# Two-layer hybrid trunk on one core: earlier activation table, MLP weights split in units of 1024 columns, weight pools by phase, odd heads' softmax transposes one step later

## The chip, the cores and the metric

The kernel runs on one core of a Trainium2 chip. The metric is the device time in microseconds (us) of one execution; lower is better. The kernel before has a median of 2300.85 us over 3 runs. PE is TensorE, DVE VectorE, ACT ScalarE, POOL GpSimd, SP the engine that issues the DMAs.

## The reference

The input x has 256 tokens of width 2048; everything is in float32. Layer 0 mixes with 8 heads of differential attention and 8 heads of a gated delta rule, layer 1 with 16 heads of dilated attention, and each layer ends in an MLP of width 8192.

```
x = x + diff_delta_mixer(rms_norm(x, ab_norm))      # layer 0: proj = h @ w_in, then heads, then @ w_out
x = x + square(relu(rms_norm(x, mlp_norm[0]) @ w1[0])) @ w2[0]
x = x + dilated_mixer(rms_norm(x, c_norm))          # layer 1
x = x + square(relu(rms_norm(x, mlp_norm[1]) @ w1[1])) @ w2[1]
```

## The kernel before, in words

**Dense products.** All products with weights go through `dense` (L189 to L211): 512 output columns (or fewer) for 256 tokens, contracted over 16 blocks `kc` of 128. PE multiplies fp32r numbers, so each fp32 weight is split: ACT rounds it to a high part (`S.copy`, L201, a CAST in the trace), DVE subtracts that from the original for the low part (`tt`, L202, shown as L107), and each `kc` takes, for either half of the tokens, three matmuls: high by high (L206), low weight by high input (L207), high weight by low input (L208). That is 96 matmuls in a dense. `wload` (L171) fetches weights in pieces of 512 KB, two `kc` each, with 4 buffers; the split parts have 6 buffers each of one `kc`, all in one pool `wp` that lives through the program.

**Phases.** Layer 0's mixer runs the denses b0, z2, bv0, b1, z0, av0, a0 and so on, one for each group of heads, then `wo`, the output product, in two parts for the two kinds of heads, over four blocks of columns (wo00 to wo03, wo10 to wo13). An MLP has 4 groups, each of 4 denses up (m_0 to m_3, by `w1`) and 4 down (n_0 to n_3, by `w2`). Behind an up dense comes relu (two ACT instructions), the square in place, 16 DVE transposes (`turn_quadrant`, L283), and the split of the result into `hh` (ACT, L314) and `hl` (DVE): n_0 needs m_3's as the last four `kc`. Layer 1's mixer has c0 to c7 and cv0 to cv3, a head pair e0 to e7 for each c, and the output product co. In the trace an MLP dense m_0 stands for every m of index 0, whatever its layer and group.

**The order of the work.** The work beside the denses is written as generators in three queues, "g", "s" and "o". `drip()` (L182) takes one step of "g" or "s", in turn, after each `kc` of a dense, and one of "o" after every fourth. A `yield` in a generator so moves what follows it two `kc` on. The instructions of each engine are then ordered by the scheduler of the language from this program order, the weight casts ahead of others (`tc.high_priority`).

**The norm.** `stats_block` (L247) sums the squares of x on ACT; `rstd` is applied to the products, so it is wanted only at the end of the first dense. `xt_block` (L257) turns x by 8 PE transposes for 512 columns (`xa0` to `xa3` at the start, `xb3`, `xc3`, `xd3` for the last block at the later phase starts, where the other blocks come during the phase before), and splits it into `xh` and `xl`.

**Heads of layer 1.** `c_side` (L1019) takes one head pair through norm, transposes, scores, softmax (`sm`), PE transposes of the softmax (`e1pt`) with a copy on ACT, and the product with v (`e1po`). Even pairs run in queue "g", odd ones in "s" (L1111).

Of the kernel before, what the change touches and what calls it, by code (L numbers as in the profile page):

```python
# [19 lines left out]
P = 128  # L20
# [11 lines left out]
AHEAD = 60  # L32
# [55 lines left out]
def trunk(  # L88
# [5 lines left out]
    V, S, G, E = nc.vector, nc.scalar, nc.gpsimd, nc.tensor  # L94

    cp = ctx.enter_context(tc.tile_pool(name="cp", bufs=1))
    sp = ctx.enter_context(tc.tile_pool(name="sp", bufs=2))
    wp = ctx.enter_context(tc.tile_pool(name="wp", bufs=6))
    xp = ctx.enter_context(tc.tile_pool(name="xp", bufs=4))
    dp = ctx.enter_context(tc.tile_pool(name="dp", bufs=1, space=bass.MemoryType.DRAM))  # L100
    psd = ctx.enter_context(tc.tile_pool(name="psd", bufs=4, space=PSUM))
# [4 lines left out]
    def tt(o, a, b, op):  # L106
        V.tensor_tensor(out=o, in0=a, in1=b, op=op)  # L107
# [13 lines left out]
    def act(o, a, f, scale=1.0, bias=0.0, accum=None):  # L121
        if accum is None:
            S.activation(out=o, in_=a, func=f, scale=scale, bias=bias)  # L123
        else:
            S.activation(out=o, in_=a, func=f, scale=scale, bias=bias, accum_out=accum)
# [7 lines left out]
    def ps_m(name):  # L133
        return psm.tile([P, 512], F32, tag="m", name=name)
# [34 lines left out]


    def wload(wsrc, k0, nm):  # L171
        raw = wp.tile([P, 2, 512], F32, tag="wr", name=f"{nm}r{k0}", bufs=4)
        off = 0
        for s in wsrc:
            m = s.shape[1]
            nc.sync.dma_start(raw[:, :, off:off + m], s[k0 * P:(k0 + 2) * P, :].rearrange("(c p) n -> p c n", p=P))
            off += m
        return raw
# [7 lines left out]
            step("o")  # L186
        tick[0] += 1

    def dense(wsrc, stat, kcs, nm, pre=(), every=1):  # L189

        n = sum(s.shape[1] for s in wsrc)
        ps = [psd.tile([P, 512], F32, tag="d", name=f"{nm}p{h}") for h in range(NH)]
        first, last = kcs[0], kcs[-1]
        for j, kc in enumerate(kcs):
            if j % 2 == 0:
                raw = pre[j // 2] if j // 2 < len(pre) else wload(wsrc, kc, nm)
            w = raw[:, j % 2, :n]
            wh = wp.tile([P, 512], F32R, tag="wh", name=f"{nm}h{kc}")[:, :n]
            wl = wp.tile([P, 512], F32R, tag="wl", name=f"{nm}l{kc}")[:, :n]
            with tc.high_priority(offset=AHEAD):  # L200
                S.copy(wh, w)  # L201
                tt(wl, w, wh.bitcast(F32), ALU.subtract)  # L202
            for h in range(NH):
                sh, sl = stat(kc, h)
                o = ps[h][:, :n]
                E.matmul(o, lhsT=sh, rhs=wh, start=kc == first, stop=False)  # L206
                E.matmul(o, lhsT=sh, rhs=wl, start=False, stop=False)  # L207
                E.matmul(o, lhsT=sl, rhs=wh, start=False, stop=kc == last)  # L208
            if j % every == 0:
                drip()  # L210
        return ps  # L211
# [7 lines left out]
    KC16 = list(range(16))  # L219
# [8 lines left out]
    ident = cst("ident")  # L228
# [74 lines left out]
    def mlp(layer, blocks, hp, done):  # L303
        w1, w2 = mlp_w1[layer], mlp_w2[layer]
        stat = stat_of(blocks)

        def spread(r, nm, hb):
            hT = hp.tile([P, 4, T], F32, tag="hT", name=nm + "hT", bufs=2)
            for i in range(4):
                turn_quadrant(r, hT, i)  # L310
                yield
            hh = hp.tile([P, 4, T], F32R, tag="hh", name=nm + "hh")
            hl = hp.tile([P, 4, T], F32R, tag="hl", name=nm + "hl")
            S.copy(hh, hT)  # L314
            tt(hl, hT, hh.bitcast(F32), ALU.subtract)
            hb.append((hh, hl))
            yield

        for g in range(4):
            hb = []  # L320
            for b in range(4):
                nm = f"m{layer}_{g}_{b}"
                c0 = (g * 4 + b) * 512
                ps = dense([w1[:, c0:c0 + 512]], stat, KC16, nm)
                r = hp.tile([P, NH, 512], F32, tag="hr", name=nm + "r", bufs=2)
                for h in range(NH):
                    act(r[:, h, :], ps[h], AF.Relu, scale=rstd[:, h:h + 1])
                act(r, r, AF.Square)
                streams["s"].append(spread(r, nm, hb))
            hstat = stat_of(hb)  # L330
            for n in range(4):
                ps = dense([w2[g * 2048:(g + 1) * 2048, n * 512:(n + 1) * 512]], hstat, KC16, f"n{layer}_{g}_{n}")
                add_to_x(n, ps)
                if g == 3:
                    done(n)
# [13 lines left out]
    warm = sp.tile([P, 512], F32, tag="junk", name="warm")  # L349
    V.memset(warm, 0.0)  # L350
    pw = ps_m("pw")
    for n in range(NWARM):
        E.matmul(pw[:, :P], lhsT=warm[:, :P], rhs=warm[:, :P], start=True, stop=True)
    xq = [x_tile(n, "xq") for n in range(4)]
    pre = []
    for n in range(4):
# [7 lines left out]
        if n < 3:  # L364
            pre.append(wload(b_cols(0), 2 * n, "b0"))
    with ExitStack() as mix:
        op = mix.enter_context(tc.tile_pool(name="op", bufs=1))
        mp = mix.enter_context(tc.tile_pool(name="mp", bufs=1))

# [11 lines left out]
        for n in range(4):  # L381
            for _ in xt_block(xq[n], n, 0, f"xa{n}", xb):
                pass


        cga = cp.tile([P, NH, 2, 64], F32, name="cga")
# [12 lines left out]
                    tt(sg[:, h, qk, hd:], rt[:, h, 1, :], g1, ALU.mult)  # L399

        def init():
            for n in range(4):
                stats_block(xq[n], n, f"xas{n}")
                yield
            stats_end("xast")
            ts(rhalf, rstd, 0.5, None, ALU.mult)
# [552 lines left out]
        ps = dense([win[:, 6920:7184]], xstat, KC16, "z2", every=2)  # L959
# [11 lines left out]
        ps = dense([win[:, 6144:6656]], xstat, KC16, "z0")  # L971
# [7 lines left out]
        ps = dense([win[:, 6656:6920]], xstat, KC16, "z1", every=2)  # L979
# [24 lines left out]


    cb = []
    with tc.tile_pool(name="hp0", bufs=6) as hp:
        mlp(0, nb, hp, lambda n: streams["s"].append(next_norm(n, 2, f"xc{n}", cb, hp)))


    cin = c_w_in[0]
    cstat = stat_of(cb)
    with ExitStack() as mix:
        op1 = mix.enter_context(tc.tile_pool(name="oq", bufs=1))
        mp1 = mix.enter_context(tc.tile_pool(name="mq", bufs=1))
        oc = [None] * 8
# [2 lines left out]
        def c_side(r, s, nm):  # L1019
            w = "gs"[s % 2]  # L1020
# [21 lines left out]
            for e in range(2):  # L1042
# [61 lines left out]
        for s in range(8):  # L1104
            ps = dense([cin[:, s * 256:(s + 1) * 256], cin[:, 2048 + s * 256:2304 + s * 256]], cstat, KC16, f"c{s}")
# [6 lines left out]
            if s % 2 == 0:  # L1112
                g = s // 2
# [24 lines left out]
        for h in range(NH):  # L1138
            nc.sync.dma_start(ov[:, h, n * 512:(n + 1) * 512], xs[n][:, h, :])

    with tc.tile_pool(name="hp1", bufs=6) as hp:
        mlp(1, nb1, hp, done1)


# [23 lines left out]
```

## Time and profile before

| | us |
|---|---|
| median of 3 runs (2300.76 to 2300.91) | 2300.85 |
| profiled execution, device time | 2301.12 |
| its span in the trace | 2299.3 |
| PE busy | 2280.7 |
| DVE busy | 1732.9 |
| ACT busy | 1275.7 |

The span is the time from the first to the last event of the trace; the profiled execution's device time lies 1.8 above it. The busy times of the engines overlap. PE's granted clock shows as 9 in all 40 slices of the page, so any lower clock is short.

### The profile page before, as it was taken

How to read it: one execution, taken by the hardware profiler on the slowest of the kernel's cores; microseconds unless marked ns; L12 is line 12 of the kernel's file. 1: busy time of each engine (PE TensorE's matmuls, PEld its weight loads, DVE VectorE, ACT ScalarE, POOL GpSimd, SP SyncE). 2: the span in 40 equal slices, each digit the busy share in tenths (PEclk: the TensorE clock that was granted, in tenths of full speed). 3: DMA queues.
4: the chain of work that ended last, by engine and by line, in shares of the span. 5: the costliest groups of instructions: out<-in, count | busy, mean ns of one | idle time of the engine just before them, and what ended most of it. 6: DMA issues, size and time to landing. Idle time of an engine off the chain costs nothing.

```text
span 2299.3 us, 31489 instructions
## 1 busy us (share of the span) xinstructions
PE 2280.7 (99%) x10536; PEld 1889.1 (82%) x10536; DVE 1732.9 (75%) x3539; ACT 1275.7 (55%) x2376; POOL 5.6 (0%) x15
## 2 busy tenths in 40 slices
PE   9999999999999999999999999999999999999999
PEld 8888888788888888888888888888888888888887
DVE  6768787867857857857898888987775775775774
ACT  6656756765545545545555565556554554554553
POOL 0000000000000000000000000000000000000000
PEclk9999999999999999999999999999999999999999
DMA  7655464566666666666656555555666666666665
GB/s 251 179 172 167 142 182 140 160 183 182 202 192 183 202 194 188 196 194 189 194 187 201 177 167 174 174 178 177 193 193 193 193 192 193 188 197 194 183 211 163
DMA packets 264775, 426.65 MB, mean 186 GB/s; under 512 B 22514, under 2 KB 94372, under 8 KB 264612
## 3 DMA queue, kind: packets, MB, share of 16 engines
q1 hardware_dynamic: 255812, 420.04, 59.9%
q10 hardware_dynamic: 8800, 4.60, 0.8%
q8 instruction: 82, 1.34, 0.2%
q14 instruction: 81, 0.66, 0.1%
HBM read 420.11 MB, written 4.46 MB: 185 GB/s over the span
## 4 chain that ended last, share of the span: by engine, by line
PE 84%; DVE 10%; ACT 2%; issue 2%; DMA 1%; ACTq 0%; SPq 0%; DVEq 0%
PE m_0p L208 3%; PE m_0p L206 3%; PE m_1p L208 3%; PE m_2p L208 3%; PE n_1p L208 3%; PE n_2p L208 3%; PE m_0p L207 3%; PE n_2p L207 3%; PE n_2p L206 3%; PE n_1p L207 3%; PE m_2p L207 3%; PE m_1p L206 3%; PE m_2p L206 3%; PE n_1p L206 3%; PE m_1p L207 3%; PE n_3p L208 3%
## 5 line engine op out<-in xcount | busy, mean ns | idle before, releaser
L107 DVE TENSOR_TENSOR n_3l<-n_3r,n_3h 128x512 fp32r<-128x512 f32 x128 | 88.3, 691 | 68.3 <-ACT n_3h L201 68.1
L107 DVE TENSOR_TENSOR n_2l<-n_2r,n_2h 128x512 fp32r<-128x512 f32 x128 | 88.2, 691 | 68.3 <-ACT n_2h L201 68.1
L107 DVE TENSOR_TENSOR m_0l<-m_0r,m_0h 128x512 fp32r<-128x512 f32 x128 | 88.4, 691 | 66.3 <-ACT m_0h L201 66.1
L201 ACT CAST n_3h<-n_3r 128x512 fp32r<-128x512 f32 x128 | 79.7, 623 | 89.3 <-DVE n_3l L107 73.6
L201 ACT CAST n_2h<-n_2r 128x512 fp32r<-128x512 f32 x128 | 79.7, 623 | 89.3 <-DVE n_2l L107 73.6
L107 DVE TENSOR_TENSOR n_1l<-n_1r,n_1h 128x512 fp32r<-128x512 f32 x128 | 87.0, 690 | 51.6 <-ACT n_1h L201 51.4
L201 ACT CAST m_0h<-m_0r 128x512 fp32r<-128x512 f32 x128 | 79.7, 623 | 81.8 <-DVE m_0l L107 61.8
L201 ACT CAST n_1h<-n_1r 128x512 fp32r<-128x512 f32 x128 | 78.9, 623 | 77.7 <-DVE n_1l L107 58.1
L201 ACT CAST m_1h<-m_1r 128x512 fp32r<-128x512 f32 x128 | 78.1, 622 | 64.6 <-PE m_1p L208 35.3
L107 DVE TENSOR_TENSOR m_1l<-m_1r,m_1h 128x512 fp32r<-128x512 f32 x128 | 87.1, 691 | 33.7 <-ACT m_1h L201 31.9
L201 ACT CAST m_3h<-m_3r 128x512 fp32r<-128x512 f32 x128 | 77.0, 621 | 47.0 <-PE m_3p L208 35.0
L201 ACT CAST m_2h<-m_2r 128x512 fp32r<-128x512 f32 x128 | 77.0, 621 | 46.8 <-PE m_2p L208 35.3
L201 ACT CAST n_0h<-n_0r 128x512 fp32r<-128x512 f32 x128 | 77.0, 621 | 46.5 <-PE n_0p L208 35.3
L107 DVE TENSOR_TENSOR m_3l<-m_3r,m_3h 128x512 fp32r<-128x512 f32 x128 | 84.9, 689 | 11.6 <-ACT m_3h L201 9.9
L107 DVE TENSOR_TENSOR m_2l<-m_2r,m_2h 128x512 fp32r<-128x512 f32 x128 | 84.9, 690 | 11.2 <-ACT m_2h L201 9.5
L107 DVE TENSOR_TENSOR n_0l<-n_0r,n_0h 128x512 fp32r<-128x512 f32 x128 | 84.9, 689 | 11.0 <-ACT n_0h L201 9.2
L289 DVE STREAM_TRANSPOSE m_0hT<-m_0r 32x256 f32<-32x256 f32 x128 | 55.8, 436 | 10.5 <-ACT m_0r L123 8.0
L289 DVE STREAM_TRANSPOSE m_1hT<-m_1r 32x256 f32<-32x256 f32 x128 | 55.8, 436 | 10.4 <-ACT m_1r L123 7.9
L289 DVE STREAM_TRANSPOSE m_3hT<-m_3r 32x256 f32<-32x256 f32 x128 | 55.8, 436 | 10.4 <-ACT m_3r L123 7.9
L289 DVE STREAM_TRANSPOSE m_2hT<-m_2r 32x256 f32<-32x256 f32 x128 | 55.8, 436 | 10.4 <-ACT m_2r L123 7.9
L208 PE MATMUL n_0p<-n_0h,m_3hl 128*128 128x512 f32 x64 | 25.8, 404 | 1.9 <-DVE m_3hl L107 1.9
L206 PE MATMUL n_0p<-n_0h,m_3hh 128*128 128x512 f32 x64 | 25.0, 390 | 0.0
(2552 smaller groups left out, 7389.0 us busy)
## 6 DMA issues: line engine op xcount, KB each, us to landing
m_0r<-in_mlp_w_dram SPq DMA_DIRECT2D x64, 512.0 KB
m_1r<-in_mlp_w_dram SPq DMA_DIRECT2D x64, 512.0 KB
m_2r<-in_mlp_w_dram SPq DMA_DIRECT2D x64, 512.0 KB
m_3r<-in_mlp_w_dram SPq DMA_DIRECT2D x64, 512.0 KB
n_0r<-in_mlp_w_dram SPq DMA_DIRECT2D x64, 512.0 KB
n_1r<-in_mlp_w_dram SPq DMA_DIRECT2D x64, 512.0 KB
n_2r<-in_mlp_w_dram SPq DMA_DIRECT2D x64, 512.0 KB
n_3r<-in_mlp_w_dram SPq DMA_DIRECT2D x64, 512.0 KB
```

Of the source, the lines that this page charges most:

```text
L107: V.tensor_tensor(out=o, in0=a, in1=b, op=op)
L201: S.copy(wh, w)
L206: E.matmul(o, lhsT=sh, rhs=wh, start=kc == first, stop=False)
L207: E.matmul(o, lhsT=sh, rhs=wl, start=False, stop=False)
L208: E.matmul(o, lhsT=sl, rhs=wh, start=False, stop=kc == last)
L289: V.transpose(out=dv[:, :, :, q], in_=sv[:, :, :, j, :])
```

## The change

1. Right after the memset of `warm`, ACT does a small Square on it (`awarm`); the activation table that it shares with the later activations is so loaded in front of it.
2. Behind the transposes of x's first block PE does 4 more matmuls into `pw`, with a result that nothing reads.
3. `init()` in queue "s" starts with two steps that do nothing, and its squares are placed behind the last weight cast issued by then (`tc.issue_after`). Everything behind `init` in "s" moves two steps on, its DMAs of constants included.
4. The MLP's denses split weights in units of 2 `kc`: CAST and subtraction of 1024 columns, with 3 buffers each instead of 6.
5. The buffers of the split weights move from `wp` to a pool of each phase: `wq0` (mixer of layer 0), `wq1` (its MLP), `wq2` and `wq3` (layer 1).
6. Odd head pairs of layer 1 yield once more in front of the transposes of the softmax.

```diff
     def wload(wsrc, k0, nm):
-        raw = wp.tile([P, 2, 512], F32, tag="wr", name=f"{nm}r{k0}", bufs=4)
+        raw = wp.tile([P, 2, 512], F32, tag="wr", name=f"{nm}r{k0}")
...
+    wq, cast = [None], [None]
+
+    def dense(wsrc, stat, kcs, nm, pre=(), every=1, unit=1):
...
-            w = raw[:, j % 2, :n]
-            wh = wp.tile([P, 512], F32R, tag="wh", name=f"{nm}h{kc}")[:, :n]
-            wl = wp.tile([P, 512], F32R, tag="wl", name=f"{nm}l{kc}")[:, :n]
-            with tc.high_priority(offset=AHEAD):
-                S.copy(wh, w)
-                tt(wl, w, wh.bitcast(F32), ALU.subtract)
+            if j % unit == 0:
+                w = raw[:, j % 2:j % 2 + unit, :n]
+                whs = wq[0].tile([P, unit, 512], F32R, tag="wh", name=f"{nm}h{kc}", bufs=6 // unit)[:, :, :n]
+                wls = wq[0].tile([P, unit, 512], F32R, tag="wl", name=f"{nm}l{kc}", bufs=6 // unit)[:, :, :n]
+                with tc.high_priority(offset=AHEAD):
+                    cast[0] = S.copy(whs, w)
+                    tt(wls, w, whs.bitcast(F32), ALU.subtract)
+            wh, wl = whs[:, j % unit], wls[:, j % unit]
...
-                ps = dense([w1[:, c0:c0 + 512]], stat, KC16, nm)
+                ps = dense([w1[:, c0:c0 + 512]], stat, KC16, nm, unit=2)
...
+    act(sp.tile([P, 16], F32, tag="rs_z", name="awarm"), warm[:, :16], AF.Square)
...
+        wq[0] = mix.enter_context(tc.tile_pool(name="wq0", bufs=1))
...
+            if n == 0:
+
+                for _ in range(4):
+                    E.matmul(pw[:, :P], lhsT=ident, rhs=xq[0][:, 1, 256:384], start=True, stop=True)
...
         def init():
+            yield
+            yield
             for n in range(4):
-                stats_block(xq[n], n, f"xas{n}")
+
+                with tc.issue_after(cast[0].ins):
+                    stats_block(xq[n], n, f"xas{n}")
                 yield
...
-    with tc.tile_pool(name="hp0", bufs=6) as hp:
+    with tc.tile_pool(name="wq1", bufs=1) as wq[0], tc.tile_pool(name="hp0", bufs=6) as hp:
...
             yield
+            if w == "s":
+                yield
             pT = mp1.tile([P, 2, 384], F32, tag="c_pT" + w, name=nm + "pT")
```

The call for `w2` gets `unit=2` too, and `wq2` and `wq3` are made like `wq0` and `wq1`.

ACT at the start, before (xas0j is the square, xa0h the rounding of x's first block, b0h the first weights; a number behind a name tells buffers apart):

```order
L125 ACT_TABLE_LOAD
L125 ACTIVATE xas0j_249,ssqp<-xq_101 128x512
L123 ACTIVATE xa0h<-xa0t_136,gt 128x256
L201 CAST b0h_229<-b0r_109 128x512
L201 CAST b0h_239<-b0r_109 128x512
L123 ACTIVATE xa0h<-xa0t_136,gt 128x256
```

ACT at the start with the change:

```order
L123 ACT_TABLE_LOAD
L123 ACTIVATE awarm<-warm 128x16
L123 ACTIVATE xa0h<-xa0t_141,gt 128x256
L123 ACTIVATE xa0h<-xa0t_150,gt 128x256
L123 ACTIVATE xa0h<-xa0t_141,gt 128x256
L204 CAST b0h_238<-b0r_111 128x512
L204 CAST b0h_248<-b0r_111 128x512
```

The table load and a small Square now stand in front, the two squares of x's first block are gone from here, and three xa0h stand ahead of the first cast instead of one.

PE where the first mixer ends (wo13, its last output block) and the first MLP begins (m_0_0), before:

```order
L208 MATMUL wo13p_5730<-wo13h_5833,d3ol 128x512
L206 MATMUL m_0_0p_5850<-m_0_0h_5854,xb0h 128x512
L207 MATMUL m_0_0p_5850<-m_0_0l_5855,xb0h 128x512
...
L207 MATMUL m_0_0p_5851<-m_0_0l_5865,xb0h 128x512
L208 MATMUL m_0_0p_5851<-m_0_0h_5864,xb0l 128x512
L231 MATMUL xb3t_5880<-ca,xs_4992 128x128 x4
L206 MATMUL m_0_0p_5850<-m_0_0h_5891,xb0h 128x512
```

The same place with the change; xb3t are the transposes of the last block of x:

```order
L212 MATMUL wo13p_5739<-wo13h_5842,d3ol 128x512
L235 MATMUL xb3t_5889<-ca,xs_5035 128x128
L235 MATMUL xb3t_5916<-ca,xs_5035 128x128
L235 MATMUL xb3t_5889<-ca,xs_5035 128x128 x3
L210 MATMUL m_0_0p_5863<-m_0_0h_5867,xb0h 128x512
L210 MATMUL m_0_0p_5864<-m_0_0h_5867,xb0h 128x512
L235 MATMUL xb3t_5916<-ca,xs_5035 128x128 x3
L211 MATMUL m_0_0p_5863<-m_0_0l_5868,xb0h 128x512
L212 MATMUL m_0_0p_5863<-m_0_0h_5867,xb0l 128x512
L211 MATMUL m_0_0p_5864<-m_0_0l_5868,xb0h 128x512
```

The transposes, which came after the 12th matmul of m_0 before, now come right behind wo13's last, with two high-by-high matmuls in their midst, and the first matmul with a low part of the weights (L211) follows them.

PE at the softmax transposes of head pair e1, before (cv1 is the dense that runs there, 12 of its matmuls follow e1pt, then e1po and the next dense c3):

```order
L208 MATMUL cv1p_13076<-cv1h_13295,xc3l 128x512
L231 MATMUL e1pt_13306<-ca,e1sm_13202 128x128 x3
L231 MATMUL e1pt_13311<-ca,e1sm_13239 128x128 x3
L206 MATMUL cv1p_13075<-cv1h_13318,xc3h 128x512
L207 MATMUL cv1p_13075<-cv1l_13319,xc3h 128x512
...
L208 MATMUL cv1p_13076<-cv1h_13332,xc3l 128x512
L1078 MATMUL e1po<-e1pT,vc_12596 128x256
L1079 MATMUL e1po<-e1pT,vc_12596 128x128
```

The same with the change:

```order
L210 MATMUL cv1p_12069<-cv1h_12314,xc3h 128x512
L211 MATMUL cv1p_12069<-cv1l_12315,xc3h 128x512
L212 MATMUL cv1p_12069<-cv1h_12314,xc3l 128x512
L235 MATMUL e1pt_12325<-ca,e1sm_12195 128x128 x3
L235 MATMUL e1pt_12330<-ca,e1sm_12232 128x128 x3
L210 MATMUL c3p_12338<-c3h_12343,xc0h 128x512
L211 MATMUL c3p_12338<-c3l_12344,xc0h 128x512
```

The transposes moved behind cv1's last 12 matmuls; c3 follows them, and e1po comes within c3. It is the same with e3 and e5.

Three more places of the changed order, in words. In n_0 DVE gets, between m_3r's square and m_3hl, 4 transposes, a subtraction of 1024 columns, 5 transposes, a subtraction, 4, one, 3, one, and then m_3hl. The first cast into a new pool waits for PE's last matmul of the phase before. At the end of the first mixer, g3's output product g3po and wo10's first matmul stand 75 rows of PE apart instead of 104, and on SP's queue three loads of wo10's weights now come ahead of the two DMAs that load blocks 2 and 3 of x again (`xs`), which wait for g3's output; DVE adds wo02 and wo03 into them, and so frees the PSUM banks that wo10 and wo11 take.

## Rows read from the trace of the kernel before

**Rows 1.** The page, section 1: busy time in us, share of the span and instructions of each engine.

```profile
PE 2280.7 (99%) x10536; PEld 1889.1 (82%) x10536; DVE 1732.9 (75%) x3539; ACT 1275.7 (55%) x2376; POOL 5.6 (0%) x15
```

**Rows 2.** PE's waits over the whole span: what waited, for what, us in total, times, the longest in us.

```profile
PE b0p L206 <- ACT b0h L201: 2.3, 1, 2.3
PE n_0p L208 <- DVE m_3hl L107: 1.9, 8, 0.2
PE e3pt L231 <- DVE e3sm L117: 1.5, 1, 1.5
PE e1pt L231 <- DVE e1sm L117: 1.5, 1, 1.5
PE e5pt L231 <- DVE e5sm L117: 1.5, 1, 1.5
...
PE bv0v L231 <- DVE bv0a L113: 1.0, 1, 1.0
...
PE g1kt L231 <- DVE g1kh L117: 0.3, 1, 0.3
```

**Rows 3.** Timeline of PE, the first matmul of some phases: z2 (the phase behind b0), m_0 and m_1 of layer 0's first group, n_0 of that group (599.67), and n_0, n_1, n_2 of the second. The columns of a timeline are start us, duration us, engine, line, operation, out<-in, shapes and count, and in brackets the engine's idle time before it and what ended that.

```profile
36.55 0.28 PE L206 MATMUL z2p<-z2h,xa0h 128*128 128x264 f32 x1
...
511.64 0.39 PE L206 MATMUL m_0p<-m_0h,xb0h 128*128 128x512 f32 x1
...
534.39 0.39 PE L206 MATMUL m_1p<-m_1h,xb0h 128*128 128x512 f32 x1
...
599.67 0.39 PE L206 MATMUL n_0p<-n_0h,m_0hh 128*128 128x512 f32 x1
...
774.29 0.39 PE L206 MATMUL n_0p<-n_0h,m_0hh 128*128 128x512 f32 x1
...
796.59 0.39 PE L206 MATMUL n_1p<-n_1h,m_0hh 128*128 128x512 f32 x1
...
818.35 0.39 PE L206 MATMUL n_2p<-n_2h,m_0hh 128*128 128x512 f32 x1
```

**Rows 4.** Timeline of the start, PE and ACT (xq is the block of x, xa0t its transposes, xas0j its square, b0h the rounded weights).

```profile
6.00 1.28 ACT L125 ACT_TABLE_LOAD   x1 [6.00 <-DMA xq<-in_x_dram]
...
6.05 0.63 PE L231 MATMUL xa0t<-ca,xq 128*128 128x128 f32 x4 [0.18 <-DMA xq<-in_x_dram]
...
7.29 0.63 ACT L125 ACTIVATE xas0j<-xq 128x512 f32<-128x512 f32 x1
...
8.28 1.12 ACT L201 CAST b0h<-b0r 128x512 fp32r<-128x512 f32 x2
...
8.94 0.79 PE L206 MATMUL b0p<-b0h,xa0h 128*128 128x512 f32 x1 [2.26 <-ACT b0h L201]
```

**Rows 5.** Windows: start:end and length in us, then busy us (and instructions) of PE, PEld, DVE, ACT and POOL, then the granted clock of PE (1.00 is 2.4 GHz), the share of the DMA engines and GB/s. One of the start, and the two that make up b0.

```profile
7.00:8.00 1.00, 0.00 (x0) 0.00 (x0) 0.00 (x0) 0.99 (x4) 0.00 (x0) 1.00 0.97 337
...
8.94:15.06 6.12, 6.12 (x16) 4.72 (x17) 4.41 (x8) 4.28 (x11) 0.00 (x0) 0.50 1.06 377
...
15.06:36.55 21.49, 21.49 (x105) 17.65 (x104) 17.28 (x62) 15.83 (x40) 0.00 (x0) 1.00 0.66 206
```

**Rows 6.** Windows, as above: the stretch before e3pt in which PE waits.

```profile
1397.35:1398.86 1.51, 0.00 (x0) 0.00 (x0) 1.40 (x6) 1.51 (x4) 0.00 (x0) 1.00 0.90 281
```

**Rows 7.** Groups by line and shape: line, engine, operation, out<-in, shapes and count, busy us and mean ns of one, and the idle time before them with what ended it. m_3l is the low part of the weights, m_3hh and m_3hl are the two parts of the squared activations, m_0hT their transpose.

```profile
L314 ACT CAST m_3hh<-m_3hT 128x1024 fp32r<-128x1024 f32 x8 | 8.4, 1053 | 24.8 <-DVE m_3hT L289 24.8
...
L107 DVE TENSOR_TENSOR m_3l<-m_3r,m_3h 128x512 fp32r<-128x512 f32 x128 | 84.9, 689 | 11.6 <-ACT m_3h L201 9.9
...
L107 DVE TENSOR_TENSOR m_3hl<-m_3hT,m_3hh 128x1024 fp32r<-128x1024 f32 x8 | 9.8, 1225 | 3.2 <-ACT m_3hh L314 3.2
...
L289 DVE STREAM_TRANSPOSE m_0hT<-m_0r 32x256 f32<-32x256 f32 x128 | 55.8, 436 | 10.5 <-ACT m_0r L123 8.0
```

**Rows 8.** Timeline of PE around e3's softmax transposes.

```profile
1396.86 0.49 PE L231 MATMUL e3pt<-ca,e3sm 128*128 128x128 f32 x3
...
1398.86 0.70 PE L231 MATMUL e3pt<-ca,e3sm 128*128 128x128 f32 x3 [1.51 <-DVE e3sm L117]
```

**Rows 9.** Timeline of PE, n_0 in the first group of layer 0, where it first needs m_3hl.

```profile
616.22 0.39 PE L207 MATMUL n_0p<-n_0l,m_3hh 128*128 128x512 f32 x1
...
616.84 0.50 PE L208 MATMUL n_0p<-n_0h,m_3hl 128*128 128x512 f32 x1 [0.24 <-DVE m_3hl L107]
```

**Rows 10.** Timeline at n_0's start in the second group: the last matmul of m_3, a weight cast on ACT, the square of m_3r.

```profile
774.06 0.39 PE L208 MATMUL m_3p<-m_3h,xb3l 128*128 128x512 f32 x1
...
774.49 0.62 ACT L201 CAST n_0h<-n_0r 128x512 fp32r<-128x512 f32 x1
...
775.73 1.06 ACT L123 ACTIVATE m_3r<-m_3r 128x1024 f32<-128x1024 f32 x1
```

**Rows 11.** Timeline at the step from the MLP of layer 0 to the mixer of layer 1, PE.

```profile
1210.88 0.39 PE L208 MATMUL n_3p<-n_3h,m_3hl 128*128 128x512 f32 x1
...
1211.10 0.39 PE L206 MATMUL c0p<-c0h,xc0h 128*128 128x512 f32 x1
```

**Rows 12.** Timelines of PE and DVE before wo10: g3's output product, DVE's second add of wo02 into xs, wo10's first matmul.

```profile
440.29 1.10 PE L766 MATMUL g3po<-g3u,g3aT 128*128 128x128 f32 x8
...
456.45 0.69 DVE L107 TENSOR_TENSOR xs<-wo02p,xs 128x512 f32<-128x512 f32 x1
...
465.18 0.39 PE L206 MATMUL wo10p<-wo10h,g2oh 128*128 128x512 f32 x1
```

More of the change, by code (lines that the diff above doesn't have):

```diff
@@ L97, in trunk @@
     sp = ctx.enter_context(tc.tile_pool(name="sp", bufs=2))
-    wp = ctx.enter_context(tc.tile_pool(name="wp", bufs=6))
+    wp = ctx.enter_context(tc.tile_pool(name="wp", bufs=4))
     xp = ctx.enter_context(tc.tile_pool(name="xp", bufs=4))
@@ L187, in drip @@
         tick[0] += 1
-    def dense(wsrc, stat, kcs, nm, pre=(), every=1):
+    wq, cast = [None], [None]
+    def dense(wsrc, stat, kcs, nm, pre=(), every=1, unit=1):
         n = sum(s.shape[1] for s in wsrc)
@@ L331, in mlp @@
             for n in range(4):
-                ps = dense([w2[g * 2048:(g + 1) * 2048, n * 512:(n + 1) * 512]], hstat, KC16, f"n{layer}_{g}_{n}")
+                ps = dense([w2[g * 2048:(g + 1) * 2048, n * 512:(n + 1) * 512]], hstat, KC16, f"n{layer}_{g}_{n}", unit=2)
                 add_to_x(n, ps)
@@ L1013, in trunk @@
     with ExitStack() as mix:
+        wq[0] = mix.enter_context(tc.tile_pool(name="wq2", bufs=1))
         op1 = mix.enter_context(tc.tile_pool(name="oq", bufs=1))
@@ L1139, in done1 @@
             nc.sync.dma_start(ov[:, h, n * 512:(n + 1) * 512], xs[n][:, h, :])
-    with tc.tile_pool(name="hp1", bufs=6) as hp:
+    with tc.tile_pool(name="wq3", bufs=1) as wq[0], tc.tile_pool(name="hp1", bufs=6) as hp:
         mlp(1, nb1, hp, done1)
```

## The prediction, on record before the change was run

> **What bounds the kernel now.** I read the page's head first: TensorE (PE) is busy for 2280.7 of 2299.3 us, so only what keeps PE from starting its next matmul counts, and time saved on VectorE (DVE, 1732.9) or ScalarE (ACT, 1275.7) counts only where PE waits for it [rows 1]. Then the list of PE's waits: the reader is to see that they are few and short, and that the largest ones lie at the start (b0p), in the attention heads (e1pt, e3pt, e5pt) and in the dense n_0 [rows 2]. The timeline gives the price of each, since a wait shows less than it costs. The steady pace is the yardstick: n_1 to n_2 start 818.35 - 796.59 = 21.76 us apart, one dense of 96 matmuls at .2266 each [rows 3]. The profiled execution took 2301.12 us, .27 above the median of 2300.85; the sum is made against 2301.12.
>
> **The start.** Before b0p, PE stands from 6.67 to 8.94, 2.26 us. The reader is to see ACT filling that time: table load from 6.00 for 1.28, the square xas0j at 7.29, the rounding of xa0, the cast at 8.28, then PE [rows 4]. In the windows the granted clock is 1.00 from 7 to 8; the 6.12 us from 8.94 on run at 0.50, that is 1.2 GHz, after that pause of 2.26, and the rest of b0 at 1.00 [rows 5]. Pauses of 1.51 us did not lower it: 1.00 in the one of e3pt [rows 6]. b0 takes 36.55 - 8.94 = 27.61 [rows 3, 4]; at full clock it would be 21.76 plus 24 transposes (xa1 to xa3) of .124. The .124 is m_0's excess, 534.39 - 511.64 - 21.76 = .99, over its 8 transposes [rows 3]. That is 24.73, so 2.88 are lost.
> The change loads the table during the first input transfer, and its ACT order is three xa0h and then the cast. The cast then waits for its data only: 512 KB at 337 GB/s is 1.5 us [rows 5], behind the x half that releases PE at 6.05 [rows 4], so 7.55. A cast of .62 [rows 10] brings the first matmul to about 8.2, and gains .7. The 4 added matmuls are like the four xa0t in .63 [rows 4]; they lie in a pause that ends with the cast, and cost nothing while the cast is later than 7.3. PE then pauses about .9 us, to 8.2, less than the 1.51 that kept the clock, so I take the 2.88 as gained too. Against this, b0's second operand and the x blocks come no earlier than their transfers: .3 by choice, as the smallest wait of that kind between engines in the list, g1kt [rows 2]. **Start: -3.3** (from -.4, with the clock lost again, to -3.6). The squares moved behind the casts (8 of .63, 5.0 us of ACT [rows 4]) are wanted only when b0 ends near 36, and z2 after it has banks of its own; if that cover failed, the next phase would wait.
>
> **Odd heads.** e3pt's first three transposes start at 1396.86 and the next at 1398.86; without a wait that would be .33 later (3 of .11, .49 for three with the tail), so 1.67 each is lost for a wait shown as 1.51 [rows 2, 8]. One more yield puts them 12 matmuls (2.7 us) later, past the softmax's end, in e1, e3 and e5 alike. The ACT copy and the product e1po behind them slip equally, into the next dense, where ACT (55% busy) has room. **-5.0** (from -4.5, the waits as shown).
>
> **MLP in units of 1024 columns.** n_0 lasts 796.59 - 774.29 = 22.30, .54 over the pace, in 8 groups [rows 3]. The cause: the first matmul with m_3hl starts at 616.84 instead of .23 after its neighbour, at 616.45 [rows 9]. The changed DVE order has, between the squared m_3r and m_3hl, 16 transposes and 4 subtractions of 1024 columns, so 16 x .436 + 4 x 1.225 + 1.225 for m_3hl itself = 13.1 [rows 7]. ACT now has a cast of 1.05 instead of .62 in front of the square, which ended at 775.73 + 1.06, so m_3r is ready near 777.25 and m_3hl near 790.4 [rows 7, 10]. PE wants it 16.78 after n_0's start (616.45 - 599.67), at 791.07 [rows 3, 9]. The wait goes, with .7 to spare: **-4.3** (8 x .54; nothing if it stays). What is late next is the pair of casts itself: the first kc of a pair is ready .43 + .53, about 1 us, later than a single one. The three buffers hold the same 6 kc, and in the order the tightest pair (the one of kc 10) keeps 1.35 us. The 8 casts and 8 subtractions saved per dense are off the bound: 0.
>
> **The pools by phase.** The first write to a new pool waits for the last reader of the old one, the last matmul. Before, c0p follows n_3p by .22 [rows 11]. Now, with T the start of that matmul, a cast begins at T+.43 (as n_0h does after m_3p [rows 10]). For m_0 of both layers the cast (1.05) is done at T+1.49, the subtraction (1.22) at T+2.77 and PE goes on at T+2.81. Meanwhile it does the tail .23, 8 transposes (.99) and 2 matmuls (.45), which the order now puts there: 1.14 lost each. For c0 in 512 columns, behind DVE's add into xs (.69 [rows 12]), PE goes on at about T+1.9 with 1.3 of work: .6. **+2.9** (from 0, if the release comes without a wait, to 6.8 if nothing fits beside: 2 x 2.58 + 1.61).
>
> **The first mixer.** All of its "s" stream slips two steps, transfers of constants included. PE's seven waits there, from bv0v's 1.0 to g1kt's .3, 4.2 in all [rows 2], may go or return elsewhere: 0, from -4.2 to +4. One place worse than before is told as a rival.
>
> Sum: -3.3 - 5.0 - 4.3 + 2.9 + 0 = -9.7, or 2301.1 - 9.7 = 2291.4 as profiled and **2291.2** against the median.
>
> **Rivals.** *The clock falls at the start anyway.* For it: it fell after 2.26 us of pause, and no row shows one of .9 there, right after PE's first few us. Then the 2.9 return: 2294.1. Beside the row stands a rule of the Trainium skill, "TensorE: Matmul & The Clock Gate", Part 1, "What's actually happening": the slow clock is the default, and a monitor grants the fast one by how busy PE has recently been. By that rule a start with few matmuls may fall back even after a short pause, and the sum would be this rival's; the trace agrees that PE's recent activity matters, with 0.50 after the pause at the start.
> *The change does not do what it says in n_0.* If the transposes or the pair of kc 12 come .7 later than worked out, the old wait stays: 2295.5.
> *New waits take back most of it.* xs is reloaded only after g3's output: in before g3po starts at 440.29, the second add into the reloaded xs at 456.45, and wo10p, which needs the bank that this add frees, at 465.18, 24.9 after g3po [rows 12]. In the changed order only 75 instead of 104 matmuls lie between, 17 us at .2266, against a chain of 16.8 (456.45 + .69 - 440.29), and three weight loads now stand ahead of the reload on SP's queue (up to 4.7 us, 3 x 512 KB at 337 GB/s [rows 5]). In time they give from nothing to 4.5 late. With the pools at their upper bound (+3.9) that is at most 2299.6, at half of both 2295.4; I take 2297.5, within .2%.
> *The pairs do not keep up, and the kernel is slower.* If the 1024-column chain comes more than the 1.35 us late, all 64 denses wait, not 8: at n_0's .54 each 34.6, of which 4.3 are paid today; the start, the heads and the pools still give -5.4, so 2301.1 + 34.6 - 4.3 - 5.4 = **2326**. For it: the chain of cast and subtraction grows from 1.3 to 2.3 us. Against it: DVE is busy 75% and gets 1.2 us back per dense, ACT 1.5 (8 x (2 x .689 - 1.225) and 8 x (2 x .62 - 1.053) [rows 7, 10]).
>
> **How the numbers follow.** What a measurement can tell from no change is .2%, 4.6 us: faster means below 2296.25. Forecast .60 (2288 to 2294); clock .17; n_0 as before .06; new waits .11; slower .06. Faster gets the forecast, n_0 and most of the clock's case, .81; within .2% the new waits and the rest, .13; slower .06. The range goes down to 2286.5 (the mixer's -4.2 and part of the pools' +2.9 saved) and up to 2299 (new waits near their bound); outside it lie the slower case and some .05 to .1 of tails.
>
> **What would show it.** Right: PEclk 1.00 from 8 to 16 and the first b0p near 8.2; no e1pt, e3pt, e5pt and no m_3hl in the list of PE's waits; n_0 at 21.8; new waits of .5 to .7 for m_0h, m_0l, c0l at the three phase starts. Wrong: a clock of 0.5 after b0p, n_0 still at 22.3, any dense of the MLP besides m_0 above 21.8, or a wait at wo10p.

## The result, and the profile after

The changed kernel takes 2304.06 us, the median of 22 runs (2299.87 to 2307.01), beside 2300.88 of the kernel before (22 runs, 2298.07 to 2302.36). The ratio is 1.0015, with a 95% interval of 1.0008 to 1.0021: a little slower, though within the .2% that the prediction counts as no change. The forecast was 2291.2, in a range to 2299.0: wrong, and on the wrong side. The profiled execution took 2305.11 us, 1.0 above the median.

PE's waits in the changed kernel (what waited for what, us in total, times, the longest) show a swap. The rows of e1pt, e3pt, e5pt and of n_0's m_3hl [rows 2] are gone, as forecast. At the head stand av1p and wo00p, denses of the first mixer that wait for the low part of their weights, and d0at and d2po of its heads; none of them stood in the list before.

```profile
PE av1p L211 <- DVE av1l L107: 3.2, 2, 2.8
PE wo00p L211 <- DVE wo00l L107: 1.9, 1, 1.9
PE d0at L235 <- DVE d0aa L113: 1.6, 2, 1.2
...
PE d2po L926 <- DVE d2mx L903: 1.1, 1, 1.1
PE b0p L210 <- ACT b0h L204: 0.8, 1, 0.8
...
PE m_0p L211 <- DVE m_0l L107: 0.4, 2, 0.2
```

The first matmuls of some phases (the timeline's columns are as in [rows 3]) give each stage its sum:

```profile
8.37 0.73 PE L210 MATMUL b0p<-b0h,xa0h 128*128 128x512 f32 x2 [0.77 <-ACT b0h L204]
...
33.98 0.28 PE L210 MATMUL z2p<-z2h,xa0h 128*128 128x264 f32 x1
...
475.81 0.39 PE L210 MATMUL wo10p<-wo10h,g2oh 128*128 128x512 f32 x1
...
611.62 0.39 PE L210 MATMUL n_0p<-n_0h,m_0hh 128*128 128x512 f32 x1
...
633.38 0.39 PE L210 MATMUL n_1p<-n_1h,m_0hh 128*128 128x512 f32 x1
...
1336.17 0.82 PE L235 MATMUL e1pt<-ca,e1sm 128*128 128x128 f32 x6
```

b0p is .57 earlier than before and z2p 2.57 [rows 3, 4]; n_0 takes 633.38 - 611.62 = 21.76, the steady pace; wo10p, at 465.18 before [rows 12], comes 10.63 later. e1pt's six transposes run in one go. With the starts of all phases compared in this way, the two traces give:

| term | forecast | in the traces |
|---|---|---|
| start, up to z2p | -3.3 | -2.6 |
| first mixer, z2p to wo10p | 0 (-4.2 to +4) | +13.2 |
| three phase starts | +2.9 | +1.34 +.87 +1.34 = +3.5 |
| n_0, 8 groups | -4.3 | 8 x -.54 = -4.3 |
| three odd head pairs | -5.0 | 3 x -1.90 = -5.7 |
| sum | -9.7 | +4.1 |

The spans differ by 2303.4 - 2299.3 = 4.1. All terms but one are within .7 us; the first mixer is off by 13.2. Two windows of PE frame it, from z2p to wo10p (columns as in [rows 5]), first of before, then of after:

```profile
36.55:465.18 428.63, 424.03 (x2273) 354.01 (x2271) 335.96 (x945) 271.92 (x662) 4.39 (x9) 1.00 0.57 169
```

```profile
33.98:475.81 441.83, 431.19 (x2273) 356.71 (x2271) 334.31 (x944) 272.11 (x661) 4.37 (x9) 0.99 0.55 164
```

Of the 13.2 us, 10.64 - 4.60 = 6.0 are idle time of PE (length less busy). PE is also busy 7.2 us longer with the same 2273 matmuls. Most of that is a lower clock behind the two largest pauses. First PE at these pauses, in av1 and in wo00, then the windows right behind them:

```profile
322.02 0.73 PE L210 MATMUL av1p<-av1h,xa2h 128*128 128x512 f32 x2 [0.46 <-ACT av1h L204]
...
325.54 0.50 PE L211 MATMUL av1p<-av1l,xa2h 128*128 128x512 f32 x1 [2.78 <-DVE av1l L107]
...
412.75 0.79 PE L211 MATMUL wo00p<-wo00l,g1oh 128*128 128x512 f32 x1 [1.88 <-DVE wo00l L107]
```

```profile
325.54:330.02 4.48, 4.48 (x13) 3.56 (x14) 4.45 (x9) 1.24 (x2) 0.00 (x0) 0.64 0.74 246
...
412.75:418.90 6.15, 6.15 (x15) 4.80 (x16) 4.16 (x9) 3.24 (x8) 0.00 (x0) 0.50 0.67 197
```

The clock was granted at .64 on average over 4.48 us and at 0.50 over 6.15: 1.6 + 3.1 = 4.7 us lost. That leaves 2.5 us of longer busy time, which no row singles out.

What is late in av1 starts on ACT. The DMAs there (ACTq) are the eight writes of the triangular solve g2 to HBM (`scx<-g2xc`, L698, L684 before); ACT takes them in its order, so it waits for the solve's result on DVE, and the weight casts stand behind it. Before:

```profile
307.71 0.62 ACT L201 CAST av1h<-av1r 128x512 fp32r<-128x512 f32 x1 [0.73 <-PE a1p L208]
...
308.50 3.44 ACTq L684 DMA_DIRECT2D scx<-g2xc  x8
...
311.99 1.27 ACT L123 ACTIVATE a1raw<-a1p,rstd 128x512 f32<-128x512 f32 x2 [3.65 <-DMA scx<-g2xc]
```

After:

```profile
312.51 0.62 ACT L204 CAST av1h<-av1r 128x512 fp32r<-128x512 f32 x1 [0.74 <-PE av1p L212]
...
317.29 3.96 ACTq L698 DMA_DIRECT2D scx<-g2xc  x8
...
321.35 1.14 ACT L204 CAST av1h<-av1r 128x512 fp32r<-128x512 f32 x2 [8.22 <-DVE d1uw L107]
```

Before, ACT went from its cast straight into the DMAs. Now it waits from 313.13 to 317.29 for the solve and then issues for nearly 4 us: 8.2 us without a cast. PE uses up the six buffers meanwhile (6 kc of 1.36 us), and waits .46 us for av1h. The longer wait, 2.78 us, ends with DVE: that cast was done at 321.97 (.62 after 321.35), but DVE's next subtraction for av1 starts at 324.80, behind steps of d1's norm. In wo00 the wait is DVE's alone. ACT casts weights of wo00 from 403.45 on, but DVE, busy without a gap from 401.03 with g3's solve and with the softmax and norm of d2 and d3, takes its next subtractions for wo00 at 412.02:

```profile
324.80 1.89 DVE L107 TENSOR_TENSOR av1l<-av1r,av1h 128x512 fp32r<-128x512 f32 x3
...
412.02 2.48 DVE L107 TENSOR_TENSOR wo00l<-wo00r,wo00h 128x512 fp32r<-128x512 f32 x4
```

The solve of g2 ends late because it starts late. Its first step on DVE, before:

```profile
296.61 0.41 DVE L113 SCALAR_TENSOR_TENSOR g2xc<-g2mb,ca 32x256 f32<-32x256 f32 x1
```

After:

```profile
306.17 0.41 DVE L113 SCALAR_TENSOR_TENSOR g2xc<-g2mb,ca 32x256 f32<-32x256 f32 x1 [2.40 <-DMA g2mb<-scm]
```

From there to the first of its DMAs it takes 11.9 us before (to 308.50) and 11.1 after (to 317.29). In PE's order g2's product g2pk stands behind 30 of a1's matmuls instead of 6. That is 4 `kc`, the two steps: the solves run in queue "g", but wait for inputs that "s" makes. The scores of d2 (d2s) stand behind 84 of a3's matmuls in both kernels. So the slip does not move all later work alike, and the solves meet other work of the heads on DVE.

The start went as forecast: no fall of the clock, with a pause of .77 before b0p. A window behind it:

```profile
9.00:10.00 1.00, 0.84 (x3) 0.30 (x2) 1.00 (x3) 0.21 (x1) 0.00 (x0) 1.00 1.00 320
```

And at a phase start, m_0 of layer 0, the order forecast with its two waits, for the last block of x and for m_0l:

```profile
523.25 0.55 PE L235 MATMUL xb3t<-ca,xs 128*128 128x128 f32 x3 [0.24 <-DVE xs L107]
...
524.90 0.50 PE L211 MATMUL m_0p<-m_0l,xb0h 128*128 128x512 f32 x1 [0.20 <-DVE m_0l L107]
```

### The profile page after: what moved, and what is told of

Its sections match the earlier page's. It is cut to its first block, busy times and chain, and to the rows that moved or that the text cites. A ratio compares the mean times of both kernels' runs of the same rounds, so it can differ in the third digit from the quotient of the medians.

```text
span 2303.4 us, 29959 instructions
## 1 busy us (share of the span) xinstructions
PE 2285.2 (99%) x10544; PEld 1891.9 (82%) x10544; DVE 1666.8 (72%) x3027; ACT 1192.3 (52%) x1865; POOL 5.6 (0%) x15
## 3 DMA queue, kind: packets, MB, share of 16 engines
q8 instruction: 82, 1.34, 0.3%
## 4 chain that ended last, share of the span: by engine, by line
PE 92%; DVE 4%; DMA 2%; ACT 1%; issue 0%; ACTq 0%; SPq 0%; DVEq 0%
PE m_0p L211 3%; PE m_0p L212 3%; PE n_0p L212 3%; PE m_1p L210 3%; PE m_3p L210 3%; PE m_2p L210 3%; PE n_1p L212 3%; PE m_3p L212 3%; PE n_2p L211 3%; PE m_1p L212 3%; PE n_1p L211 3%; PE m_2p L212 3%; PE n_0p L210 3%; PE n_2p L210 3%; PE n_2p L212 3%; PE n_1p L210 3%
## 5 line engine op out<-in xcount | busy, mean ns | idle before, releaser
L107 DVE TENSOR_TENSOR n_2l<-n_2r,n_2h 128x1024 fp32r<-128x1024 f32 x64 | 78.4, 1226 | 76.8 <-ACT n_2h L204 76.7
L107 DVE TENSOR_TENSOR n_3l<-n_3r,n_3h 128x1024 fp32r<-128x1024 f32 x64 | 78.4, 1225 | 76.7 <-ACT n_3h L204 76.6
L107 DVE TENSOR_TENSOR m_0l<-m_0r,m_0h 128x1024 fp32r<-128x1024 f32 x64 | 78.1, 1225 | 73.4 <-ACT m_0h L204 73.0
L107 DVE TENSOR_TENSOR n_1l<-n_1r,n_1h 128x1024 fp32r<-128x1024 f32 x64 | 78.4, 1224 | 67.7 <-ACT n_1h L204 67.2
L204 ACT CAST n_2h<-n_2r 128x1024 fp32r<-128x1024 f32 x64 | 67.4, 1053 | 100.3 <-PE n_2p L212 61.6
L204 ACT CAST n_1h<-n_1r 128x1024 fp32r<-128x1024 f32 x64 | 67.4, 1053 | 92.8 <-PE n_1p L212 60.0
L107 DVE TENSOR_TENSOR m_1l<-m_1r,m_1h 128x1024 fp32r<-128x1024 f32 x64 | 78.4, 1225 | 36.9 <-ACT m_1h L204 35.9
L107 DVE TENSOR_TENSOR m_3l<-m_3r,m_3h 128x1024 fp32r<-128x1024 f32 x64 | 78.4, 1225 | 25.7 <-ACT m_3h L204 24.3
L107 DVE TENSOR_TENSOR n_0l<-n_0r,n_0h 128x1024 fp32r<-128x1024 f32 x64 | 78.4, 1225 | 25.7 <-ACT n_0h L204 24.0
L107 DVE TENSOR_TENSOR m_2l<-m_2r,m_2h 128x1024 fp32r<-128x1024 f32 x64 | 78.4, 1225 | 25.7 <-ACT m_2h L204 23.8
```

The lines of the kernel that those rows point to most:

```text
L204: cast[0] = S.copy(whs, w)
```

## Experiments

The theory (A) was that the two empty steps in front of `init()` cost the 13 us: all later work of queue "s" stands two steps later against the phases, and hits places where PE's order has no room. (By the places above this holds for the solves, and not for the scores of d2.) The expectations count the loss from bv0p on, as 14.0; some work of z2 slips behind bv0p, so 13.2 from z2p on is the better figure. Ratios are to the kernel before on the same chip.

**no_slip: the change without the two steps**

```diff
         def init():
-            yield
-            yield
             for n in range(4):
```

> The changed kernel without the two empty first steps of init(); the order of the first mixer is then that of the kernel before on ACT. In the changed kernel PE was 3.4 us ahead of before at bv0p and 10.6 behind at wo10p, so the first mixer lost 14.0. Theory A (the slip of queue s by two steps causes that): about 2304.1 - 14.0 = 2290, and the waits of av1p (3.2) and wo00p (1.9) are gone. Rival B (the pools by phase or the squares behind the casts cause it): 2304 and the same waits.

Measured: 2291.58 us, ratio .9963 (.9951 to .9975). The window from z2p to wo10p:

```profile
33.87:462.88 429.01, 424.53 (x2273) 353.98 (x2271) 335.97 (x947) 272.90 (x664) 4.39 (x9) 1.00 0.57 170
```

429.01 us against 428.63 before and 441.83 with the slip. ACT again goes from a cast into the DMAs of g2 without a wait:

```profile
305.21 0.63 ACT L204 CAST av1h<-av1r 128x512 fp32r<-128x512 f32 x1 [0.72 <-PE a1p L212]
...
305.98 3.42 ACTq L696 DMA_DIRECT2D scx<-g2xc  x8
```

So the slip is the cause of the loss. The rest of the change gains most of what was forecast for it: 8.2 us against the kernel before on the same chip (2299.82), where the forecast was 9.7. That 2291.6 lies so near the forecast 2291.2 is in part luck: the chip of this run is 1 us faster with the kernel before, and the start's shortfall is made up by the odd heads.

**slip_only: the kernel before with the two steps alone**

```diff
         def init():
+            yield
+            yield
             for n in range(4):
```

> The kernel before with the two empty first steps of init() and nothing else of the change. Theory A: slower by about the 14.0 us that the first mixer lost, 2301 + 14 = 2315, with waits at av1p and wo00p. Rival B (the slip costs only together with the pools or the squares' place): 2301.

Measured: 2310.83 us, ratio 1.0053 (1.0041 to 1.0065). The same waits, in a kernel without any other part of the change:

```profile
PE av1p L207 <- DVE av1l L107: 2.7, 1, 2.7
...
PE wo00p L207 <- DVE wo00l L107: 1.9, 1, 1.9
```

11.0 us lost in the medians, 4 less than theory A's 2315. In the profiled execution z2p comes 1.2 earlier (35.40) and wo10p at 474.09: 438.69 us lie between, 10.1 more than before.

**repaid: the two steps kept, two later ones joined**

```diff
             nc.sync.dma_start(lv[:, 264:272], b_dt_bias[0].partition_broadcast(P))
-            yield
             nc.sync.dma_start(gn[:, 0:64], a_q_norm[0].partition_broadcast(P))
             nc.sync.dma_start(gn[:, 64:128], a_k_norm[0].partition_broadcast(P))
-            yield
             nc.sync.dma_start(grow[0:16, :], mlp_norm[0].rearrange("(c p) -> c p", p=P))
```

> The changed kernel, its two empty first steps of init() kept, but two later steps of init() that only issue DMAs of constants joined to the one before them, so that everything in queue s behind init stands where it stood before. Theory A (the standing slip of all later work in s against the phases costs the 14 us): 2291 to 2292 as without the two steps. Rival G (the later squares and so the later rstd cost it): 2304.

Measured: 2291.2 us, ratio .9964 (.9951 to .9976). The squares come as late as in the change (the first xas0j at 16.5 us in both, at 8.7 in no_slip), and nothing is lost. It is the standing shift of what follows in the queue.

**slip1: one step instead of two**

```diff
         def init():
             yield
-            yield
```

> The changed kernel with one empty first step of init() instead of two. If the loss grows evenly with the slip, about half of it: 2291.6 + 6.2 = 2298. If a step is free until a buffer of weights runs out at one place (av1, wo00), either 2291.6 or 2304; I expect about 2295, since the waits have slack on both sides.

Measured: 2299.42 us, ratio .9998 (.9989 to 1.0007): 8 us over no_slip, against the 12.5 of two steps. My 2295 was too low. An even growth, 2298, lies within the interval, so the time does not settle whether a step costs half. The places differ: av1 is free, wo00p waits 2.6 us for its weights and d3ot 2.3, and the granted clock falls to 0.50 behind either. The loss depends on where the late work falls.

**pool_dma: the solve's DMAs issued by POOL**

```diff
-                    nc.scalar.dma_start(
+                    nc.gpsimd.dma_start(
                         bass.AP(sxy.tensor, sxy.offset + q * 512 + i * P,
                                 [[BLK * 1024 + BLK, 8], [1024, BLK], [1, BLK]]),
                         xc[i * 8:(i + 1) * 8, q])
```

> The changed kernel with the eight small DMA writes of the triangular solve (scx from gNxc) issued by POOL instead of ACT. Theory C (within A: ACT stands 8.2 us without a weight cast, as these DMAs wait for DVE's g2xc and then take 4 us to issue, so that the weights of av1 run out and the clock falls): the waits of av1p and wo00p go with the halved clock after them, about 3.7 + 3.5 and 1.9 + 2.9, so 2304 - 12 = 2292. Rival D (DVE's load at that place sets the wait, ACT only follows): the waits stay, 2303 to 2304.

Measured: 2304.61 us, ratio 1.0021 (1.0012 to 1.0029): no gain, theory C missed. av1p's wait fell to .4, and another took its place:

```profile
PE g2lp L722 <- DMA g2xy<-scx: 2.8, 1, 2.8
PE wo00p L211 <- DVE wo00l L107: 1.9, 1, 1.9
```

The way of g2's result, on POOL (the writes), ACT's queue (the load back) and PE (the product that needs it):

```profile
316.78 5.00 POOL L698 DMA_DIRECT2D scx<-g2xc  x8 [18.86 <-DVE g2xc L128]
...
324.52 0.35 ACTq L704 DMA_DIRECT2D g2xy<-scx  x1
...
329.08 1.22 PE L722 MATMUL g2lp<-g2xy,g2mT 128*128 128x128 f32 x6 [2.84 <-DMA g2xy<-scx]
```

The product g2lp now holds PE 2.8 us, and the clock falls behind it as it did behind av1l (0.56 on average from 329.08 to 333.00). So ACT's standing was only the nearer of two late things: the solve itself is too late for the place that PE's order gives to g2lp. POOL also took 5.00 us for the eight writes, where ACT took 3.96.

**pool_dma_y and act_y: the products gNlp (g2lp among them) two steps later, with the DMAs on POOL or on ACT**

```diff
             S.copy(aT, quads(t))
-            for _ in range(4):
+            for _ in range(6):
                 yield
```

(In pool_dma_y on top of pool_dma, in act_y alone.)

> The changed kernel with the scx writes issued by POOL, as in the run pool_dma, and two more yields between the loading of gNxy and the product gNlp, so that PE meets that product 4 kc later. In pool_dma ACT cast on in time, but PE then stood 2.8 us at g2lp for the round trip of the solve through HBM. If the solve of g2 is just late against the place where PE's order expects it: that wait goes with the clock's fall there, 2304.6 - 2.8 - 3 = 2299 or less. If DVE is short of time at that place whatever waits for it: a wait at another product or at av1l takes its place, 2303 to 2305.

> The changed kernel, the scx writes issued by ACT as there, with only the two more yields before gNlp of the run pool_dma_y. If ACT's standing in order behind these DMAs was a cause by itself: the wait of av1l stays with the clock's fall behind it, 2302 to 2304. If the place of gNlp in PE's order was all of it: 2296, as in pool_dma_y.

Measured: pool_dma_y 2296.23 us, ratio .9984 (.9975 to .9993); act_y 2300.01, ratio 1.0000 (.9991 to 1.0009). The first went as the late place of g2lp would have it: no wait in av1, no lower clock in the mixer, a smaller wait in wo01:

```profile
PE wo01p L211 <- DVE wo01l L107: 2.3, 3, 1.7
```

The second missed both of its values. ACT does not stand there either, although the DMAs are its own, since their place in its order moved with the rest:

```profile
320.91 0.62 ACT L204 CAST a2h<-a2r 128x512 fp32r<-128x512 f32 x1 [0.75 <-PE av1p L212]
...
320.94 3.23 ACTq L698 DMA_DIRECT2D scx<-g2xc  x8
```

They are issued right behind a cast, at 320.94, and take 3.23 us. From z2p to wo10p act_y takes 6.0 us less than the change and 7.2 more than before:

```profile
34.39:470.18 435.79, 426.50 (x2272) 353.83 (x2271) 335.22 (x942) 271.42 (x661) 4.37 (x9) 1.00 0.56 166
```

At a clock of 1.00 PE is busy for 4.7 us less than in the change, but still for 2.5 more than before, so those 2.5 us are not the clock's. Of the 9.3 us idle, 3.9 are waits for weights in wo01, and 2.3 are five short waits at the end of wo02, where g3's products stand one behind the other. So which engine issues the DMAs is not the root, though with g2lp later the issue by POOL is some 3.5 us faster than that by ACT; what counts first is where these instructions and g2lp stand against the solve. Over no_slip 4.7 and 8.4 us remain.

**pool_one and best: the weights' pools**

pool_one puts all split weights into one pool of 3 buffers of two kc (on top of no_slip):

```diff
...
+            if j % 2 == 0:
+                whp = wq[0].tile([P, 2, 512], F32R, tag="wh", name=f"{nm}h{kc}", bufs=3)
+                wlp = wq[0].tile([P, 2, 512], F32R, tag="wl", name=f"{nm}l{kc}", bufs=3)
             if j % unit == 0:
-                w = raw[:, j % 2:j % 2 + unit, :n]
+                u = slice(j % 2, j % 2 + unit)
+                w, whs, wls = raw[:, u, :n], whp[:, u, :n], wlp[:, u, :n]
...
```

> The kernel without the slip, with the split weights in one pool of 3 buffers of two kc for the whole program instead of a pool for each phase (in the mixers each half of such a buffer is cast by itself). The three phase starts showed +1.3, +.9 and +1.3 in the changed kernel; if the pools cause that: 2291.6 - 3.5 = 2288, and m_0p follows wo13p at .23. Rival (the last adds into x would hold the transposes anyway): 2291.6. In the mixers a buffer comes free two kc at a time, which may cost a little.

Measured: 2292.49 us, ratio .9969 (.9957 to .9980). The three starts gave -1.35, -.87 and -1.34, as expected, but the mixer lost 4.2 up to wo10p, at wo00 and wo01 above all. PE waits there 1.4 us for DVE's d2aa and .6 for d2mx, and the clock falls to 0.50 behind them, at 407.44; whether the buffers, which come free only two kc at a time, are behind that is not shown. best keeps buffers of one kc in a pool for the whole program, for the mixers and the first dense of each MLP:

```diff
+    wqg = ctx.enter_context(tc.tile_pool(name="wqg", bufs=1))
...
-                whs = wq[0].tile([P, unit, 512], F32R, tag="wh", name=f"{nm}h{kc}", bufs=6 // unit)[:, :, :n]
+                whs = (wm if unit == 2 else wq)[0].tile([P, unit, 512], F32R, tag="wh", name=f"{nm}h{kc}", bufs=6 // unit)[:, :, :n]
...
-                ps = dense([w1[:, c0:c0 + 512]], stat, KC16, nm, unit=2)
+                ps = dense([w1[:, c0:c0 + 512]], stat, KC16, nm, unit=1 if g == b == 0 else 2)
...
```

(`wm` is the pool of the MLP, `wq` now the one of the whole program.)

> The kernel without the slip; the split weights of one kc stay in one pool for the whole program, which the mixers and the first dense of each MLP use, and only the other MLP denses take units of two kc from a pool of their MLP. If the first cast into a new pool causes the loss at the three phase starts, they show +0 against before instead of +1.3, +.9 and +1.3, without the loss that pool_one showed at wo00: 2291.6 - 3.5 = 2288. If the transposes of the last block of x would wait there anyway: 2291.6.

Measured: 2287.94 us, ratio .9948 (.9935 to .9960), the fastest of all. The last matmul of a phase and the first of the next are .23 apart again:

```profile
508.24 0.39 PE L213 MATMUL wo13p<-wo13h,d3ol 128*128 128x512 f32 x1
...
508.47 0.39 PE L211 MATMUL m_0p<-m_0h,xb0h 128*128 128x512 f32 x1
...
1205.56 0.39 PE L213 MATMUL n_3p<-n_3h,m_3hl 128*128 128x512 f32 x1
...
1205.78 0.39 PE L211 MATMUL c0p<-c0h,xc0h 128*128 128x512 f32 x1
```

**unit1, no_odd and no_mm2: one part undone each, without the slip**

unit1 drops `unit=2` from both calls in `mlp`; no_odd drops the yield of `if w == "s"`; no_mm (with the slip) and no_mm2 (without it) drop the four added matmuls.

> The kernel without the slip, with the MLP's weights split in units of 512 columns again and the pools by phase kept. The prediction's term: n_0 waits for m_3hl again, 8 x .54 = 4.3, less about 2 x .5 at the two starts of an MLP, where a cast of 512 columns is ready earlier: 2291.6 + 4.3 - 1 = 2295. Rival (the units do nothing, the waits went by the pools): 2291.6.

> The kernel without the slip and without the additional yield of the odd heads. The prediction's term -5.0, and 3 x 1.90 = 5.7 by the trace of the changed kernel: 2291.6 + 5 to 5.7 = 2297, with waits of 1.5 at e1pt, e3pt and e5pt. Rival (the waits would go anyway with the lighter DVE): 2291.6.

> The changed kernel without the four added matmuls of the start. Theory E (they keep the granted clock): PE's pause before b0p grows from 0.8 to about 1.3, the clock falls as in the kernel before and b0 takes 2.9 longer, 2307. Rival F (the shorter pause is enough, from the early table): no change, 2304.

> The kernel without the slip and without the four added matmuls of the start. The run without them but with the slip showed the clock at 0.50 after a pause of 1.44 us, and yet the same time. If that was hidden by the mixer's waits and their spread: here b0 takes 2.9 longer, 2291.6 + 1.5 to 3 = 2293 to 2294.5 (the clock was back after 11 us there, earlier than in before). If the mixer takes it up in any case: 2291.6.

Measured: unit1 2294.7 us, ratio .9979 (.9970 to .9988), 3.1 over no_slip, where its phases show +.54 to +.57 in each of 8 n_0 and -.43 at each start of an MLP. no_odd 2297.67, ratio .9991 (.9982 to 1.0000), 6.1 over no_slip, with the waits back:

```profile
PE e3pt L235 <- DVE e3sm L117: 1.5, 1, 1.5
PE e5pt L235 <- DVE e5sm L117: 1.5, 1, 1.5
PE e1pt L235 <- DVE e1sm L117: 1.5, 1, 1.5
```

no_mm 2303.9, ratio 1.0021 (1.0012 to 1.0029), no difference to the change; no_mm2 2292.87, ratio .9968 (.9955 to .9980), 1.3 over no_slip in medians, with ranges that touch (2291.25 to 2294.97 beside 2290.52 to 2292.15), so that a gain by the four matmuls is likely and not settled. In no_mm, PE's first matmul of b0 and a window behind it:

```profile
8.24 1.22 PE L210 MATMUL b0p<-b0h,xa0h 128*128 128x512 f32 x2 [1.44 <-ACT b0h L204]
```

```profile
9.00:10.00 1.00, 1.00 (x4) 0.81 (x3) 0.91 (x2) 0.08 (x1) 0.00 (x0) 0.50 1.08 352
```

In no_mm2:

```profile
8.88 0.50 PE L210 MATMUL b0p<-b0h,xa0h 128*128 128x512 f32 x1 [1.44 <-ACT b0h L204]
```

```profile
9.00:10.00 1.00, 1.00 (x4) 0.47 (x4) 1.00 (x2) 1.00 (x3) 0.00 (x0) 1.00 1.08 345
```

The same pause of 1.44 us, and the clock is 0.50 behind it in one execution and 1.00 in the other. The wait at wo00p shows it with the same work around it: it is 1.88 us in the change and in no_mm, and behind it the clock was 0.50 for 6.15 us in the change, while in no_mm it stays at 1.00:

```profile
412.15 0.50 PE L211 MATMUL wo00p<-wo00l,g1oh 128*128 128x512 f32 x1 [1.88 <-DVE wo00l L107]
```

```profile
412.15:418.30 6.15, 6.15 (x27) 5.09 (x28) 4.16 (x9) 3.56 (x9) 0.00 (x0) 1.00 0.69 208
```

In that execution the stretch from z2p to wo10p lasts 437.69 us, 9.1 more than before and not 13.2.

## Why the prediction was wrong

- **The first mixer** is the step that failed: "PE's seven waits there ... may go or return elsewhere: 0, from -4.2 to +4". It measured +13.2. I bounded the slip by the waits that the kernel before shows, as if a slip could do no more than undo or double them. But that kernel shows no wait at av1 or wo00 because its solves end where there is room. The bound had to come from the work that is moved: eight DMAs on ACT that wait for DVE and take nearly 4 us, the casts behind them, the steps that come before weight subtractions on DVE, and the 8.2 us that six buffers last. The clock's price behind pauses of 1.9 and 2.8 us, 4.7 us in the profiled execution, was counted at the start of the kernel only. That the slip is the cause is shown by no_slip, slip_only and repaid. That the solve of g2 is late for its place is shown by pool_dma and pool_dma_y. It is late by its start, not by its length (11.1 us beside 11.9): steps of d1's norm now run between its own, but do not make it longer. How av1, wo00 and g3's products share the loss was not taken apart by runs, and the 2.5 us of longer busy time stay open.
- **The start**: the mechanism held (b0p at 8.37, clock 1.00); -2.6 instead of -3.3, as b0 gained 2.0 and not 2.6. The rival of a falling clock did not come true here. The Trainium skill ("TensorE: Matmul & The Clock Gate", Part 1, "What's actually happening") calls the warm-up run-variable, the same kernel giving different counts of slow matmuls. The 22 runs of the change agree that the clock differs from run to run: the mean granted clock goes from .997 (2307.01 us) to 1.000 (2300.55).
- **Odd heads** and **n_0**: right, -5.7 for -5.0 and -4.3 for -4.3; no_odd and unit1 give them back. That the pairs would not keep up (the slower rival) is refuted: no dense of an MLP but the first m_0 of each is above 21.8.
- **The pools**: right in place and nearly in size, +3.5 for +2.9; best takes the loss away. The waits look different from those forecast: .2 us each, for m_0l, c0h and the last block of x, instead of .5 to .7.
- **wo10 behind the reload of xs**, in which I put the danger of the slip: PE does not wait there, wo10p follows wo03p by 11.84 us, 11.65 before. It was the wrong place of the right part.

## What to carry to other kernels

A step put in front of a queue moves what follows in it, and work of other queues that waits for it, but not all work alike: price the moved work at its new place, the DMAs in an engine's order and what stands behind them first, then the engine that must prepare the next operands, and not by the waits that the old place shows. Where an order of work is tuned, pay a shift back within the queue (repaid) before counting on any gain. A pause on the engine that bounds a kernel costs more than its length if the clock falls behind it.

## What the runs showed that I had not expected

The granted clock does not follow the length of a pause alone: it fell behind pauses of 2.26 us (before), 1.88 and 2.78 (after), and behind 1.44 in no_mm, and it held behind 1.44 in no_mm2, 1.51 in e3pt, 1.88 in wo00 of no_mm and 2.00 in wo01 of act_y. Whether such falls also widen the spread is not settled: no_mm goes over 6.4 us in 10 runs and unit1, whose profile shows none, over 2.6 in 10; but pool_dma, with two falls, goes over 3.9 in 11 and act_y, with none, over 4.7 in 11.
